# Turning the last results of a row-wise cosine similarity into rows with block transposes, and awaiting the stores at the last barrier

## The chip, the cores and the metric

The kernel runs on one core of a Trainium2 chip. The time is the device time of one execution in microseconds (us), as a median over runs; "span" is the length of a profiled execution from its first to its last instruction, 1.8 to 2.0 us shorter than the time. In this text PE is TensorE, DVE is VectorE, ACT is ScalarE, POOL is GpSimd and SP is the Sync engine; a "q" behind a name (SPq) means an instruction that the engine's sequencer handles by itself. A "mark" of an engine is a value of its semaphore that others wait for.

## The reference

```python
def setup_inputs():
    return {
        "x": np.random.randn(8192, 8192).astype(np.float32),
        "y": np.random.randn(8192, 8192).astype(np.float32),
    }

def reference(x, y):
    x_norm = np.linalg.norm(x, axis=1, keepdims=True)
    y_norm = np.linalg.norm(y, axis=1, keepdims=True)
    return np.sum(x * y, axis=1) / (x_norm.squeeze() * y_norm.squeeze() + 1e-8)
```

Two matrices of 268 MB each are read once; 8192 numbers are written.

## The kernel before

Rows lie on partitions. ScalarE squares and sums (`square`), VectorE multiplies and sums (`dot`). A loop takes the first 7680 rows in 30 groups of 256; then come four blocks of 128 rows (`NB = 4`), the last of them cut into 13 pieces so that little is left to do when its last piece lands. Every row's result is at first one number on its own partition, a column of 128; to be stored in long pieces it must become a row. The parts that matter here:

```python
    def dot(a, b, acc, into, init=0.0):
        return nc.vector.tensor_tensor_reduce(
            out=into, in0=a, in1=b, scale=1.0, scalar=init, op0=ALU.mult, op1=ALU.add,
            accum_out=acc)
# ... for the pieces of a block:
                chained = b == last and n == len(pieces[b]) - 1
                if not chained:
                    acc = parts[:, XX if p.which == "x" else YY, p.i:p.i + 1]
                    xy, init = parts[:, XY, p.i:p.i + 1], 0.0
                else:                      # the very last piece starts from the sum of the others
                    dve.wait(*marks)
                    m_base = dve.done(nc.vector.tensor_reduce(
                        out=base, in_=parts, axis=AX.X, op=ALU.add))
                    acc, xy, init = fin, bsum[:, XY, b:b + 1], base[:, XY:XY + 1]
# ... after the pieces: norms of the last block on ScalarE, then
        pe.wait(identity, m_dot)
        m_xy = pe.done(nc.tensor.transpose(out=psl[0], in_=bsum[:, XY, :], identity=ident))
        act.wait(m_xy)
        m_dots = act.done(nc.scalar.copy(out=dots, in_=psl[0]))
        dve.wait(m_xn, m_yn)
        mk = dve.done(nc.vector.tensor_scalar(            # the denominator
            out=bden[:, last:], in0=bnorm[:, 1, last:], scalar1=bnorm[:, 0, last:],
            scalar2=EPS, op0=ALU.mult, op1=ALU.add))
        dve.wait(mk)
        mk = dve.done(nc.vector.reciprocal(out=bden[:, last:], in_=bden[:, last:]))
        pe.wait(m_den, mk)
        mk = pe.done(nc.tensor.transpose(out=psl[1], in_=bden, identity=ident))
        dve.wait(mk, m_dots)
        mk = dve.done(nc.vector.tensor_mul(out=orl, in0=psl[1], in1=dots))
        sp.wait(mk)
        stored_last = (sem("stored_last"), 16)
        nc.sync.dma_start(
            out=out.rearrange("(t p) -> t p", p=P)[nt - NB:, :], in_=orl).then_inc(
                stored_last[0], 16)
        sp.wait(stored, stored_last)
```

A function that runs over the finished program moves that last wait to the head of the closing block, in which the engines meet at two barriers and GpSimd clears the semaphores between them.

## Time and profile before

| before | |
|---|---|
| time, median of 3 runs | 1249.45 us (1249.18 to 1249.65) |
| span of the profiled run | 1247.6 us |
| read from HBM | 536.87 MB, 430 GB/s over the span |
| VectorE, ScalarE busy | 56%, 73% |
| last load landed | 1243.07 us |
| from there to the end, "the tail" | 4.51 us |

How to read it: the DMA row of the page stands at 9 (90% or more) in every slice but the last, and no engine is near 100%. The loads set the time up to the landing of the last piece. Only the tail is left for a change of this kind, so I measure everything from the last landing; the landing itself moves between 1242.8 and 1243.6 us from profile to profile, and hides changes of a few tenths in the total time.

Two lines will matter later. The first is the last store's issue, from the view of the output tensor (duration in ns: least, median, most); it was known when predicting. The second, from the view of the line that ends the body, is Sync's drain behind it, whose length the prediction does not use. The line above it is a NOP, Sync's last record in the body; its last start, 1246.2, serves as a cut through the tail later.

```profile
L384 SPq DMA_DIRECT2D out_dram<-orl x1: 348/348/348, 1245.4 to 1245.4; - x1
```

```profile
L168 SPq NOP  x2: 13/16/18, 0.8 to 1246.2; - x2
L168 SPq DRAIN  x1: 90/90/90, 1245.9 to 1245.9; - x1
```

The issue takes 0.35 us, and Sync passes its drain 0.09 us after reaching it.

### The profile page before, as it was taken

How to read it: one execution, taken by the hardware profiler on the slowest of the kernel's cores; microseconds unless marked ns; L12 is line 12 of the kernel's file. 1: busy time of each engine (PE TensorE's matmuls, PEld its weight loads, DVE VectorE, ACT ScalarE, POOL GpSimd, SP SyncE). 2: the span in 40 equal slices, each digit the busy share in tenths (PEclk: the TensorE clock that was granted, in tenths of full speed). 3: DMA queues.
4: the chain of work that ended last, by engine and by line, in shares of the span. 5: the costliest groups of instructions: out<-in, count | busy, mean ns of one | idle time of the engine just before them, and what ended most of it. 6: DMA issues, size and time to landing. Idle time of an engine off the chain costs nothing. (4 is left out here: it accounts for less than half of the span.)

```text
span 1247.6 us, 1785 instructions
## 1 busy us (share of the span) xinstructions
PE 1.3 (0%) x4; PEld 0.3 (0%) x4; DVE 698.2 (56%) x252; ACT 916.9 (73%) x285; POOL 0.8 (0%) x8
## 2 busy tenths in 40 slices
PE   0000000000000000000000000000000000000000
PEld 0000000000000000000000000000000000000000
DVE  1654576545765447654467544675446755457566
ACT  3686776867768668677686776867868668677888
POOL 0000000000000000000000000000000000000000
DMA  9999999999999999999999999999999999999998
GB/s 435 431 414 435 437 437 437 437 435 435 433 412 437 437 437 437 437 437 435 435 424 420 437 437 437 437 437 437 433 433 412 437 437 437 437 437 437 418 425 335
DMA packets 11575, 536.93 MB, mean 430 GB/s; under 512 B 1299, under 2 KB 1845, under 8 KB 2613
## 3 DMA queue, kind: packets, MB, share of 16 engines
q1 hardware_dynamic: 11528, 536.88, 99.6%
q10 hardware_dynamic: 45, 0.03, 0.0%
q14 instruction: 2, 0.02, 0.0%
HBM read 536.87 MB, written 0.03 MB: 430 GB/s over the span
## 5 line engine op out<-in xcount | busy, mean ns | idle before, releaser
L142 ACT ACTIVATE junk<-slot 128x8192 uint8<-128x8192 f32 (+4 forms) x138 | 900.8, 6528 | 326.2 <-ACTq L139 320.5
L145 DVE CUSTOM_DVE_ANT_0 slot<-slot,slot 128x4096 f32<-128x4096 f32 (+1 forms) x60 | 391.1, 6556 | 452.4 <-DVEq L139 452.4
L212 DVE COPY side<-slot 128x4096 f32<-128x4096 f32 x30 | 132.8, 4428 | 71.7 <-DVEq L139 71.7
L145 DVE CUSTOM_DVE_ANT_0 side<-side,slot,part 128x4096 f32<-128x4096 f32 x30 | 134.6, 4488 | 0.0
L145 DVE CUSTOM_DVE_ANT_0 slot<-slot 128x8192 f32<-128x8192 f32 (+3 forms) x5 | 29.6, 5944 | 20.4 <-ACT junk L142 12.7
L142 ACT ACTIVATION_READ_ACCUMULATOR junk<-slot (+1 forms) x138 | 25.7, 186 | 0.0
L145 DVE CUSTOM_DVE_ANT_0 vjunk<-slot 128x384 uint8<-128x384 f32 (+4 forms) x8 | 6.8, 886 | 1.0 <-DMA slot<-in_y_dram 1.0
L145 DVE DVE_READ_ACCUMULATOR2_ANT gsum<- x60 | 6.7, 112 | 0.0
L145 DVE DVE_READ_ACCUMULATOR2_ANT part<- 128x1 f32 x30 | 2.5, 83 | 0.0
L192 ACT ACT_TABLE_LOAD x1 | 1.3, 1283 | 1.0 <-SPq L168 1.0
L350 PE MATMUL side<-ident,gden 128*30 128x128 f32 x2 | 0.6, 395 | 1196.9 <-DVE gden L344 1196.9
L194 ACT ACT_TABLE_LOAD x1 | 1.3, 1283 | 0.1
L145 DVE DVE_READ_ACCUMULATOR2_ANT parts<- 128x1 f32 x11 | 0.9, 82 | 0.0
L353 DVE COPY orow<-side 30x128 f32<-30x128 f32 x2 | 0.5, 279 | 0.6 <-PE side L350 0.6
L371 ACT COPY dots<-side 4x128 f32<-4x128 f32 x1 | 0.3, 254 | 0.7 <-PE side L369 0.7
L145 DVE CUSTOM_DVE_ANT_0 vjunk<-slot,base 128x384 uint8<-128x384 f32 x1 | 0.6, 619 | 0.1
L381 DVE TENSOR_TENSOR orl<-side,dots 4x128 f32<-4x128 f32 x1 | 0.3, 279 | 0.5 <-PE side L379 0.5
L270 DVE RECIPROCAL gden<-gden 128x60 f32<-128x60 f32 x1 | 0.5, 529 | 0.0
L350 PEld LDWEIGHTS side<-ident,gden 128*30 128x30 f32 x2 | 0.1, 107 | 1196.8 <-issue 1196.8
L369 PE MATMUL side<-ident,bsum 128*4 128x128 f32 x1 | 0.4, 373 | 46.9 <-DVE bsum L145 46.9
L379 PE MATMUL side<-ident,bden 128*4 128x128 f32 x1 | 0.4, 374 | 0.0
L340 ACT ACTIVATE gnorm<-gsum 128x120 f32<-128x120 f32 x1 | 0.3, 302 | 0.0
(25 smaller groups left out, 4.4 us busy)
## 6 DMA issues: line engine op xcount, KB each, us to landing
slot<-in_x_dram SPq DMA_DIRECT2D x3, 4096.0 KB, 29.9
slot<-in_y_dram SPq DMA_DIRECT2D x2, 4096.0 KB, 32.2
slot<-in_y_dram SPq DMA_DIRECT2D x1, 2368.0 KB, 35.8
slot<-in_x_dram SPq DMA_DIRECT2D x1, 1984.0 KB, 32.3
slot<-in_y_dram SPq DMA_DIRECT2D x1, 1728.0 KB, 39.4
slot<-in_y_dram SPq DMA_DIRECT2D x1, 1600.0 KB, 35.7
slot<-in_x_dram SPq DMA_DIRECT2D x1, 1088.0 KB, 37.9
slot<-in_y_dram SPq DMA_DIRECT2D x1, 640.0 KB, 40.2
```

The costliest lines, as they stand in the source:

```text
L142: return nc.scalar.activation(out=into, in_=src, func=ACTF.Square, accum_out=acc)
L145: return nc.vector.tensor_tensor_reduce(out=into, in0=a, in1=b, scale=1.0, scalar=init, op0=ALU.mult, op1=ALU.add, accum_out=acc)
L192: nc.scalar.memzero(dummy).then_inc(squared, 1)
L194: nc.scalar.sqrt(out=dummy, in_=dummy).then_inc(squared, 1)
L212: nc.vector.tensor_copy(out=side, in_=xt[:, CUT:])
L270: return dve.done(nc.vector.reciprocal(out=den, in_=den))
L340: m_norm = act.done(nc.scalar.activation(out=gnorm, in_=flat(gsum)[:, 0:2], func=ACTF.Sqrt))
L350: mk = pe.done(nc.tensor.transpose(out=t, in_=gden[:, j:2 * G:2], identity=ident))
L353: rows.append(dve.done(nc.vector.tensor_copy(out=orow[:, :, j], in_=t)))
L369: m_xy = pe.done(nc.tensor.transpose(out=psl[0], in_=bsum[:, XY, :], identity=ident))
L371: m_dots = act.done(nc.scalar.copy(out=dots, in_=psl[0]))
L379: mk = pe.done(nc.tensor.transpose(out=psl[1], in_=bden, identity=ident))
```

## The change

Its intent is to shorten the tail: no trip through TensorE and PSUM for the last results, the three earlier blocks out of the way before the tail, no reduction in front of the last dot, and the store's landing awaited beside the closing barriers and not ahead of them. The core of the diff (cut where marked):

```diff
-    closing = blocks[-1]
+    waits = []
     for b in blocks:
# ... collects the waits for "stored" from all blocks
+    closing = list(blocks[-1].instructions)
+    at = max(n for n, i in enumerate(closing)
+             if i.opcode == "Drain" and i.engine == waits[0].engine)
+    blocks[-1].instructions = closing[:at] + waits + closing[at:]
# ...
+    bcol = sb.tile([P, NB, TB], FP32, name="bcol")          # TB = 32
+    brow = sb.tile([P, NB, TB], FP32, name="brow")
+    stored = nc.alloc_semaphore("stored")                   # one for all three stores
# ...
+        def store_blocks(a, b):
+            dve.wait(m_bcol)
+            m = dve.done(nc.vector.tensor_mul(
+                out=bcol[:, a:b, 0], in0=bsum[:, XY, a:b], in1=bden[:, a:b]))
+            dve.wait(m)
+            m = dve.done(nc.vector.transpose(
+                out=brow[:, a:b].rearrange("p b i -> p (b i)"),
+                in_=bcol[:, a:b].rearrange("p b i -> p (b i)")))
+            sp.wait(m)
+            nc.sync.dma_start(
+                out=out.rearrange("(t q i) -> q t i", i=TB, q=P // TB)[
+                    :, nt - NB + a:nt - NB + b],
+                in_=brow[0:P:TB, a:b]).then_inc(stored, 16)
# ... the chained last dot goes; all pieces are summed by one reduction
-                    m_den = reciprocal(bnorm[:, :, 0:last], bden[:, 0:last], m_norm, m_sum)
-            if b in manys and b != last:
+                    reciprocal(bden[:, 0:last], bnorm[:, :, 0:last], m_norm)
+                    store_blocks(0, last)
+            if b in manys:
# ... at the end: both transposes on TensorE, the copy and the multiply by rows go
+        dve.wait(dve.done(nc.vector.reciprocal(out=bden[:, last:], in_=bden[:, last:])))
+        store_blocks(last, NB)
+        take(nc.sync, stored, 48)
```

A block transpose of a column puts 32 of its values in a row on partitions 0, 32, 64 and 96: the store reads `brow[0:P:TB]`.

More of the change, by code (lines that the diff above doesn't have):

```diff
@@ L28, in first_load_and_last_wait @@
     opening.instructions = head[:at] + [load] + head[at:]
-    closing = blocks[-1]
+    waits = []
     for b in blocks:
-        waits = [i for i in b.instructions
-                 if i.sync_info and any(
-                     "stored" in (w.ant_name or "") for w in i.sync_info.on_wait)]
-        if waits:
-            b.instructions = [i for i in b.instructions if i.name not in {w.name for w in waits}]
-            closing.instructions = waits + list(closing.instructions)
+        own = [i for i in b.instructions
+               if i.sync_info and any(
+                   "stored" in (w.ant_name or "") for w in i.sync_info.on_wait)]
+        if own:
+            waits += own
+            b.instructions = [i for i in b.instructions if i.name not in {w.name for w in own}]
+    assert waits
+    closing = list(blocks[-1].instructions)
+    at = max(n for n, i in enumerate(closing)
+             if i.opcode == "Drain" and i.engine == waits[0].engine)
+    blocks[-1].instructions = closing[:at] + waits + closing[at:]
 class Queue:
@@ L87 @@
     CUT = 2 * K - SIDE
+    TB = 32
     xg = x[0:G * 2 * P, :].rearrange("(r a p j) k -> r a p (j k)", a=SLOTS, p=P, j=2)
@@ L117 @@
     bden = sb.tile([P, NB], FP32, name="bden")
-    base = sb.tile([P, 3], FP32, name="base")
-    fin = sb.tile([P, 1], FP32, name="fin")
+    bcol = sb.tile([P, NB, TB], FP32, name="bcol")
+    brow = sb.tile([P, NB, TB], FP32, name="brow")
     ident = sb.tile([P, P], FP32, name="ident")
@@ L122 @@
     orow = sb.tile([G, P, 2], FP32, name="orow")
-    dots = sb.tile([NB, P], FP32, name="dots")
-    orl = sb.tile([NB, P], FP32, name="orl")
     def sem(name):
         return tc.alloc_semaphore(name)
+    stored = nc.alloc_semaphore("stored")
     landed = [sem(f"landed{s}") for s in range(SLOTS)]
@@ L256, with reciprocal @@
             if ny > 1:
-                m = max(len(pieces[b]) - ny, ny - 1 if b == NB - 1 else ny)
+                m = max(len(pieces[b]) - ny, ny)
                 parts = sb.tile([P, 3, m], FP32, name=f"parts{b}")
                 manys[b] = parts, pool.done(nc.gpsimd.memset(parts, 0.0))
+        m_bcol = pool.done(nc.gpsimd.memset(bcol, 0.0))
         ring = {"A": Ring(junk, act), "V": Ring(vjunk, dve)}
-        def reciprocal(norm, den, squared, dotted):
-            dve.wait(squared, dotted)
+        def reciprocal(den, norm, *marks):
+            dve.wait(*marks)
             m = dve.done(nc.vector.tensor_mul(out=den, in0=norm[:, 0], in1=norm[:, 1]))
@@ L269, in reciprocal @@
             dve.wait(m)
-            return dve.done(nc.vector.reciprocal(out=den, in_=den))
+            dve.wait(dve.done(nc.vector.reciprocal(out=den, in_=den)))
+        def store_blocks(a, b):
[11 more added lines that the diff above has]
+                in_=brow[0:P:TB, a:b]).then_inc(stored, 16)
         def flat(t):
@@ L293 @@
             for n, p in enumerate(pieces[b]):
-                chained = b == last and n == len(pieces[b]) - 1
-                if not chained:
-                    acc = parts[:, XX if p.which == "x" else YY, p.i:p.i + 1]
-                    xy, init = parts[:, XY, p.i:p.i + 1], 0.0
-                else:
-                    dve.wait(*marks)
-                    m_base = dve.done(nc.vector.tensor_reduce(
-                        out=base, in_=parts, axis=AX.X, op=ALU.add))
-                    acc, xy, init = fin, bsum[:, XY, b:b + 1], base[:, XY:XY + 1]
+                acc = parts[:, XX if p.which == "x" else YY, p.i:p.i + 1]
+                xy = parts[:, XY, p.i:p.i + 1]
                 zero = [m_zero] if m_zero else []
@@ L315 @@
                     dve.wait(p.mark, *zero, *[q[0] for q in xmarks],
-                             *([q[1] for q in xmarks] if over else []),
-                             *([m_base] if chained else []))
+                             *([q[1] for q in xmarks] if over else []))
                     if over:
-                        mk_dot = dve.done(dot(p.x, p.src, xy, p.x, init))
+                        mk_dot = dve.done(dot(p.x, p.src, xy, p.x))
                     else:
-                        mk_dot = ring["V"].done(
-                            dot(p.x, p.src, xy, ring["V"].room(p.w), init))
+                        mk_dot = ring["V"].done(dot(p.x, p.src, xy, ring["V"].room(p.w)))
                     marks.append(mk_dot)
-                if chained:
-                    m_fin, m_dot = mk, marks[-1]
                 if b == last and n == 4:
@@ L341 @@
                     out=gnorm, in_=flat(gsum)[:, 0:2], func=ACTF.Sqrt))
-                m_g = reciprocal(gnorm, gden, m_norm, marks[-1])
-                dve.wait(m_g)
+                reciprocal(gden, gnorm, m_norm)
                 m_g = dve.done(nc.vector.tensor_mul(
@@ L353 @@
                     rows.append(dve.done(nc.vector.tensor_copy(out=orow[:, :, j], in_=t)))
-                stored = (sem("stored_groups"), 16)
             if b == 2:
@@ L358 @@
                     out=out[0:G * 2 * P].rearrange("(g q) -> g q", q=2 * P),
-                    in_=orow.rearrange("g p j -> g (p j)")).then_inc(stored[0], 16)
-        psl = [side[0:NB, j * BANK:j * BANK + P] for j in range(2, 4)]
-        act.wait(m_base)
-        m_xn = act.done(nc.scalar.activation(
-            out=bnorm[:, 0, last:], in_=base[:, XX:XX + 1], func=ACTF.Sqrt))
-        act.wait(m_fin)
-        m_yn = act.done(nc.scalar.activation(
-            out=bnorm[:, 1, last:], in_=fin, func=ACTF.Sqrt, bias=base[:, YY:YY + 1]))
-        pe.wait(identity, m_dot)
-        m_xy = pe.done(nc.tensor.transpose(out=psl[0], in_=bsum[:, XY, :], identity=ident))
-        act.wait(m_xy)
-        m_dots = act.done(nc.scalar.copy(out=dots, in_=psl[0]))
-        dve.wait(m_xn, m_yn)
-        mk = dve.done(nc.vector.tensor_scalar(
+                    in_=orow.rearrange("g p j -> g (p j)")).then_inc(stored, 16)
+        act.wait(m_sum)
+        m_norm = act.done(nc.scalar.activation(
+            out=bnorm[:, :, last], in_=bsum[:, 0:2, last], func=ACTF.Sqrt))
+        dve.wait(m_norm)
+        m = dve.done(nc.vector.tensor_scalar(
             out=bden[:, last:], in0=bnorm[:, 1, last:], scalar1=bnorm[:, 0, last:],
             scalar2=EPS, op0=ALU.mult, op1=ALU.add))
-        dve.wait(mk)
-        mk = dve.done(nc.vector.reciprocal(out=bden[:, last:], in_=bden[:, last:]))
-        pe.wait(m_den, mk)
-        mk = pe.done(nc.tensor.transpose(out=psl[1], in_=bden, identity=ident))
-        dve.wait(mk, m_dots)
-        mk = dve.done(nc.vector.tensor_mul(out=orl, in0=psl[1], in1=dots))
-        sp.wait(mk)
-        stored_last = (sem("stored_last"), 16)
-        nc.sync.dma_start(
-            out=out.rearrange("(t p) -> t p", p=P)[nt - NB:, :], in_=orl).then_inc(
-                stored_last[0], 16)
-        sp.wait(stored, stored_last)
+        dve.wait(m)
+        dve.wait(dve.done(nc.vector.reciprocal(out=bden[:, last:], in_=bden[:, last:])))
+        store_blocks(last, NB)
+        take(nc.sync, stored, 48)
 _INS = ['x', 'y']
```

## The prediction

> **What bounds the kernel now.** I read the page's engine row and slices first, then the table of stretches, then the timeline of the last microseconds, then the Sync engine's waits, and last the single semaphore records of the final barrier.
>
> ```profile
> DMA  9999999999999999999999999999999999999998
> HBM read 536.87 MB, written 0.03 MB: 430 GB/s over the span
> core 0: us, PE busy (x) PEld busy (x) DVE busy (x) ACT busy (x) POOL busy (x), PEclk, DMA share, GB/s
> 0.00:1200.00 1200.00, 0.58 (x2) 0.14 (x2) 668.48 (x218) 878.21 (x250) 0.80 (x8) 1.00 1.00 433
> 1232.00:1243.00 11.00, 0.00 (x0) 0.00 (x0) 9.97 (x20) 10.74 (x19) 0.00 (x0) 1.00 0.90 348
> 1243.00:1248.00 5.00, 0.70 (x2) 0.16 (x2) 1.59 (x8) 1.29 (x6) 0.00 (x0) 1.00 0.00 0
> ```
>
> Loads fill the transfer engines for 1243 of the 1247.6 us: DMA share 1.00 at 433 GB/s up to 1200, while VectorE is busy 56% and ScalarE 73% of the span. The change touches no load, no slot and none of the loop's instructions. Whatever it is worth must therefore lie after the last load lands, in the 4.5 us with DMA share 0.00. That tail is 0.36% of the time, so a change of 2% (25 us) isn't to be had there in either direction.
>
> The tail is a serial chain. Its VectorE and TensorE part, from the timeline:
>
> ```profile
> 1242.66 0.55 DVE L145 CUSTOM_DVE_ANT_0 vjunk<-slot 128x384 uint8<-128x384 f32 x1
> 1243.14 0.08 DVE L145 DVE_READ_ACCUMULATOR2_ANT parts<- 128x1 f32 x1
> 1243.33 0.17 DVE L300 TENSOR_REDUCE base<-parts 128x3 f32<-128x21 f32 x1
> 1243.64 0.62 DVE L145 CUSTOM_DVE_ANT_0 vjunk<-slot,base 128x384 uint8<-128x384 f32 x1
> 1244.33 0.37 PE L369 MATMUL side<-ident,bsum 128*4 128x128 f32 x1 [46.88 <-DVE bsum L145]
> 1244.74 0.25 ACT L371 COPY dots<-side 4x128 f32<-4x128 f32 x1 [0.70 <-PE side L369]
> 1245.09 0.28 DVE L381 TENSOR_TENSOR orl<-side,dots 4x128 f32<-4x128 f32 x1 [0.50 <-PE side L379]
> 1245.40 0.35 SPq L384 DMA_DIRECT2D out_dram<-orl  x1
> ```
>
> The last piece's semaphore completes at 1243.071 (landing record). VectorE is then at the end of its self-dot of the last x piece, does the reduction, and only then the last dot, which needs the reduction as its starting value. Transposes on TensorE, a copy, a multiply and the store follow. After the store, from the Sync engine's waits and the summary of the barrier's line:
>
> ```profile
> SPq L55 <- DMA out_dram<-orl: 0.4, 1, 0.4
> L414 POOLq EVENT_SEMAPHORE_RANGE_CLEAR  x1: 222/222/222, 1247.1 to 1247.1; - x1
> ```
>
> Sync stands 0.4 us for the store to land, and only then enters the first of two closing barriers. Between the two, GpSimd clears the semaphores.
>
> **What the Trainium skill says.** "VectorE: DVE Perf Modes", section "The three transpose paths": VectorE transposes 32x32 blocks only, and into SBUF, while TensorE's full transpose goes to PSUM. Before has only the TensorE kind: 0.37 us each, plus 0.25 us for the copy out of PSUM. The same page, "The TRN2 errata", gives (N+151)/0.96 ns for an fp32 two-input operation: 160 ns for 3 elements, 220 for 60. The trace has 159 ns for the multiply of 3 and 0.22 us for that of 60, so it agrees. "Perfetto Trace Analysis", "DMA Instruction — HWDGE", says that the data movement lies outside the issue's recorded window and that confirmation from HBM can take surprisingly long. Here the issue takes 0.348 us and the landing comes 1.203 us after its start (1245.401 to 1246.604). "DMA: Bandwidth & Descriptors", "Specifications", says that pieces under 512 B are read, modified and written. The store before is 4 rows of 512 B; the new last store is 4 rows of 128 B, which no run has shown yet.
>
> **The change part by part.**
>
> 1. *One sum over all pieces.* The last dot no longer waits for the reduction. It needs its data (1243.071) and VectorE, free for the next dot at 1243.14 (the dots before it start 0.48 us apart, as each hands over to its accumulator read). It starts at 1243.14 and not 1243.64: 0.50 earlier. Its sum is out 0.57 later (1242.660 to 1243.234 for its neighbour), at 1243.71; ScalarE's last square is out at 1243.718. The reduction now stands behind both. In the trace it starts 0.09 after the mark that it waits for and signals 0.19 later, so 1243.81 to 1244.00. Then comes one Sqrt of 2 elements for two of 1: 0.02 to start, 0.19 to signal, 1244.21. Before, the second Sqrt had signalled at 1244.044, and VectorE could begin the denominator when the dot was done, at 1244.189. Now it begins at about 1244.24: this part alone gives 0.05 us back.
>
> 2. *Block transposes.* Before, from the denominator's start to the store's issue: 1245.401 - 1244.189 = 1.21 us (scalar operation, reciprocal, TensorE transpose, VectorE multiply). The ScalarE copy of the other transpose ran beside it and ended last (signal 1245.001). Now: scalar operation 0.22 to its signal, reciprocal 0.02 + 0.18, multiply of one column 0.02 + 0.17 (the multiply of 3 takes 159 ns), transpose of 32 elements, start of the issue 0.02. The formula above gives 183/0.96 = 191 ns for 32 elements; I allow 0.22 for filling the block, plus 0.03 to start. Sum 0.22 + 0.20 + 0.19 + 0.25 + 0.02 = 0.88. Issue at 1244.24 + 0.88 = 1245.12, against 1245.40: **0.28 us saved by parts 1 and 2.**
>
> 3. *Three blocks stored on their own.* This adds on VectorE, near 1238.3, a multiply (0.16 + 0.02) and a transpose of 96 elements (247/0.96 = 257 ns, with fill and start 0.31): about 0.5 us in front of the dot of 1280 that began at 1238.15. VectorE sat idle 0.53 us before 1240.15 and 0.43 before 1241.67, both for y pieces, so the delay is absorbed before the tail. The store's 12 rows go behind the loads already issued on the same queue and land near 1243, more than 2 us before the last store is issued.
>
> 4. *Where the stores are awaited.* By the order of the instructions, the wait moves from ahead of both closing barriers to just before Sync's arrival at the second. Sync's last action before it is recorded at 1246.182; the store wait runs at 1246.620, and Sync's next record follows at 1246.688. The other engines need 0.08 to 0.11 us from their corresponding record to their first one in the closing block. So Sync without the wait gets there at about 1246.28, 0.41 earlier. What follows no longer depends on the landing, provided the landing comes before GpSimd is ready at the second barrier. That is 0.54 us after its first release (1246.859 to 1247.401). Counted from the store's issue: first release at +1.05 (1.458 before, less 0.41), GpSimd ready at +1.59; landing at +1.20 and 0.1 us for Sync to react, +1.30. Slack 0.29 us. **0.41 us saved.**
>
> Sum: 0.28 + 0.41 = 0.69 us; 1249.45 - 0.69 = 1248.76, say **1248.8 us**.
>
> **The rivals.**
>
> - *The small rows land late.* If writing 128 B costs more than 0.29 us over 512 B, the second barrier waits for the landing and part of the 0.41 goes: with 0.7 us more, all of it. For it: the page's remark on 512 B. Against: the store's packets took 0.025 us each, and most of the 1.20 us is issue (0.35), start (0.43) and confirmation. Time then 1249.0 to 1249.2.
> - *The chain grows rather than shrinks.* The reduction, Sqrt and two extra VectorE steps are now in series behind the last dot. If the transpose took 0.5 us and each hand-over 0.05 more, parts 1 and 2 would be a loss of about 0.2: 1249.2. Against it: the durations of these sizes are all in the trace, but for the transpose.
> - *VectorE falls behind before the tail.* The added 0.5 us would need a VectorE without gaps from 1238 on; it has 0.96 us of them, so I give this little. It would cost up to 0.3.
> - *Nothing is seen.* The transfers set 1243 us of the time, and the three runs of before spread over 0.47 us (1249.18 to 1249.65). A gain of 0.69 is not far above that, so the difference of medians could come out anywhere from 0.3 to 1.1 faster.
>
> **Range and chances.** The working's own error is about 0.25 us (the transpose's duration, Sync's jump to its closing block, the landing), and the runs add about 0.2 of spread. Leaning towards the rivals, which nearly all cost time, I take 1248.3 to 1249.3. Within 2% is all but certain, as the whole tail is 4.5 us: 0.99.
>
> **What would show it right or wrong.** In the changed profile the last dot should start 0.0 to 0.1 us after the accumulator read of the x self-dot; the 32-element transpose should take 0.19 to 0.25 us; the last store should be issued about 2.05 us after the last landing (before 2.33), and the span should end about 1.77 us after that issue (before 2.18). A Sync wait on the store's landing that ends after GpSimd is ready for the second barrier would show the first rival. An idle time of zero on VectorE before its last four dots would show the third. A load stretch that changes by more than 0.5 us would make the prediction wrong in a way that I didn't work out.

## The result, and the profile after

The changed kernel takes 1249.32 us (median of 6 runs, 1249.14 to 1249.42), the kernel before 1249.43 us (6 runs, 1249.18 to 1249.65). The ratio is 0.9999 with a 95% interval of 0.9986 to 1.0012: the same. The prediction had 1248.8 and a range of 1248.3 to 1249.3; the measured time lies just outside. As the landing of the last piece alone moves by several tenths, the distance to the edge of the range says little; the tail says more.

The stretches show that the loads are untouched and that the tail is still idle of transfers (columns as in the prediction's first fence):

```profile
0.00:1200.00 1200.00, 0.58 (x2) 0.14 (x2) 668.41 (x218) 878.48 (x250) 0.94 (x9) 1.00 1.00 433
1232.00:1243.00 11.00, 0.00 (x0) 0.00 (x0) 10.44 (x22) 10.73 (x19) 0.00 (x0) 1.00 0.88 341
1243.00:1248.00 5.00, 0.00 (x0) 0.00 (x0) 1.67 (x9) 0.96 (x5) 0.00 (x0) 1.00 0.00 0
```

The 0.47 us more of VectorE between 1232 and 1243 are the early multiply and transpose. They are absorbed as foreseen, as the timeline shows: the dot of 1280 begins at 1238.76 (before 1238.15), and the next one at 1240.22 (before 1240.15, after a wait for its data).

```profile
1238.36 0.17 DVE L283 TENSOR_TENSOR bcol<-bsum,bden 128x3 f32<-128x3 f32 x1
1238.56 0.28 DVE L286 STREAM_TRANSPOSE brow<-bcol 128x96 f32<-128x96 f32 x1
1238.76 1.45 DVE L150 CUSTOM_DVE_ANT_0 vjunk<-slot 128x1280 uint8<-128x1280 f32 x1
...
1240.22 1.09 DVE L150 CUSTOM_DVE_ANT_0 vjunk<-slot 128x896 uint8<-128x896 f32 x1
```

The timeline of the tail, from the last dot on (the last piece landed at 1243.118):

```profile
1243.18 0.55 DVE L150 CUSTOM_DVE_ANT_0 vjunk<-slot 128x384 uint8<-128x384 f32 x1
...
1243.85 0.18 DVE L347 TENSOR_REDUCE bsum<-parts 128x3 f32<-128x24 f32 x1
1244.06 0.21 ACT L373 ACTIVATE bnorm<-bsum 128x2 f32<-128x2 f32 x1 [0.30 <-DVE bsum L347]
1244.30 0.21 DVE L376 TENSOR_SCALAR bden<-bnorm 128x1 f32<-128x1 f32 x1 [0.27 <-ACT bnorm L373]
1244.55 0.16 DVE L380 RECIPROCAL bden<-bden 128x1 f32<-128x1 f32 x1
1244.75 0.16 DVE L283 TENSOR_TENSOR bcol<-bsum,bden 128x1 f32<-128x1 f32 x1
1244.94 0.21 DVE L286 STREAM_TRANSPOSE brow<-bcol 128x32 f32<-128x32 f32 x1
1245.18 0.55 SPq L290 DMA_DIRECT2D out_dram<-brow  x1
```

The chain of compute is as predicted: the store is issued 2.06 us after the last landing (predicted 2.05, before 2.33). But its own line has grown from 0.35 to 0.55 us, and Sync's drain behind it, in the view of the line that ends the body, from 90 to 397 ns:

```profile
L173 SPq NOP  x2: 13/16/18, 0.8 to 1246.5; - x2
L173 SPq DRAIN  x1: 397/397/397, 1245.9 to 1245.9; - x1
```

Sync's waits no longer hold a wait of 0.4 us for the last store (the row that the prediction shows has no counterpart); the wait is at the second barrier and finds the stores landed.

The tail can be cut at two of Sync's records: the start of the last store's issue, and Sync's last record ahead of the closing block (the last start of the NOP in the lines above, by which Sync has heard from all engines; here with three decimals from the records themselves). The three stretches add up to the tail:

| us | landing to issue | issue to NOP | NOP to end | tail |
|---|---|---|---|---|
| before | 2.330 | 0.781 | 1.403 | 4.514 |
| after | 2.063 | 1.295 | 0.956 | 4.314 |
| difference | -0.267 | **+0.514** | -0.447 | -0.200 |

The first and the third stretch gained what was foreseen, 0.71 us together. The second one, which the prediction carried over unchanged from the kernel before, took back 0.51. One caution on the first stretch: the kernel before stands in it with a single profile, and four runs below whose code is the same up to the issue (e1, e3, e8, e12) show 2.289 to 2.298, so some 0.035 us of the 0.267 may be chance.

### The profile page after: what moved, and what is told of

Same layout as the page of the kernel before. It is cut to its first block, busy times and chain, and to the rows that moved or that the text cites. A ratio compares the mean times of both kernels' runs of the same rounds, so it can differ in the third digit from the quotient of the medians.

```text
span 1247.4 us, 1781 instructions
## 1 busy us (share of the span) xinstructions
PE 0.6 (0%) x2; PEld 0.1 (0%) x2; DVE 698.6 (56%) x255; ACT 916.6 (73%) x283; POOL 0.9 (0%) x9
```

## The experiments

**Theory A.** The last store has become dear to issue, because its rows lie 32 partitions apart. In the program as it is built, a DMA instruction can carry a mark, a field whose name (`ant_dge_precooked`) speaks of a prepared form. (From here on, "mark" is this field, and not a semaphore's value.) All loads and both stores of the kernel before carry it. Of the changed kernel's DMAs, just the two stores of blocks don't. Building the store in other shapes, without running them, showed where the mark is set: on rows on adjoining partitions (4 rows of 512 or of 128 B, 3 rows, 128 rows of 4 B), and not on rows 2, 32 or 64 partitions apart.

**Rivals.** B: pieces of 128 B in place of 512 B are slow to issue or to land. C: the store is the second on its queue and shares its semaphore with others, and waits for them. A further question was whether the moved wait and the single sum are worth what I reckoned.

The table holds every run's three stretches; the text after it takes them up one by one. Times are medians of the runs, for e9 and e10 of a single one. The kernel before had 1249.44 in the rounds of e1 to e4, 1249.61 in those of e5, e6, e8 and the changed kernel's repeat, and 1249.29 in those of e9 to e12; the three groups ran on three chips. By the verdict at 2% every one of these kernels is "same" (e9 and e10 have no verdict); what tells them apart is the tail. Each tail is read from one profile. Where several profiles hold the same code, landing to issue agrees to about 0.04 us and the stretches behind it to less than 0.02.

| us | landing to issue | issue to NOP | NOP to end | tail | time |
|---|---|---|---|---|---|
| after, again | 2.026 | 1.300 | 0.957 | 4.283 | 1249.67 |
| e1 mark off | 2.289 | 1.458 | 1.303 | 5.050 | 1250.06 |
| e2 rows from partitions 0 to 3 | 2.047 | 0.793 | 0.956 | 3.796 | 1248.78 |
| e3 wait only | 2.296 | 0.785 | 0.956 | 4.037 | 1249.05 |
| e12 the same again | 2.298 | 0.780 | 0.956 | 4.034 | 1248.99 |
| e4 column store | 1.824 | 0.752 | 6.451 | 9.027 | 1253.84 |
| e5 chained | 2.152 | 1.300 | 0.957 | 4.409 | 1249.52 |
| e9 chained, wait later | 1.966 | 1.295 | 0.956 | 4.217 | 1249.28 |
| e6 one store | 2.144 | 1.407 | 0.957 | 4.508 | 1249.32 |
| e8 two marks off | 2.294 | 1.441 | 1.303 | 5.038 | 1250.17 |
| e10 early store marked | 2.059 | 1.384 | 0.956 | 4.399 | 1249.45 |
| e11 by quadrants | 2.533 | 0.795 | 0.956 | 4.284 | 1249.55 |

The changed kernel was run once more as the reference of e5, e6 and e8, and gave the same tail to 0.03 us; its time was 0.35 us longer than in its first six runs. In the two profiled runs, 0.43 us apart, the last load landed 0.46 us later (1243.58 us), which covers the difference.

> The changed kernel once more, as the reference of the three runs beside it on this chip. Tail from the last landing to the end 4.31 us as in its first profile, last store's issue 0.55 us, time 1249.3.

### e1: the kernel before, without the mark on its last store

```diff
+    last = [i for b in blocks for i in b.instructions if i.opcode == "DMACopy"][-1]
+    for b in blocks:
+        b.instructions = [copy.replace(i, ant_dge_precooked=False) if i.name == last.name
+                          else i for i in b.instructions]
```

> The kernel before with one bit changed: the last store (4 rows of 512 B from partitions 0 to 3) loses the mark for the prepared form of issue that the build gives it. Theory A (the changed kernel's last store is slow because its rows lie 32 partitions apart and so has no mark): Sync's issue rises from 0.35 to about 0.55 us, Sync's drain behind it from 0.09 to about 0.40, the landing comes about 1.6 us after the start of the issue (before 1.20), the tail grows by 0.4 us, time about 1249.8. Rival B (rows of 128 B are the cause) and rival C (a second store on the same queue and the shared semaphore): nothing changes, 1249.4.

Nothing else differs: same rows of 512 B, same partitions, one store on the queue. The result is correct and took 1250.06 us (4 runs, 1249.92 to 1250.21; before in the same rounds 1249.44, 1249.11 to 1249.94). The view of the output tensor, and that of the line that ends the body:

```profile
L390 SPq DMA_DIRECT2D out_dram<-orl x1: 757/757/757, 1245.3 to 1245.3; - x1
```

```profile
L174 SPq DRAIN  x1: 352/352/352, 1246.2 to 1246.2; - x1
```

The issue takes 0.76 us in place of 0.35 and the drain 0.35 in place of 0.09; issue to NOP 1.46 in place of 0.78, and the landing comes 1.78 us after the start of the issue in place of 1.20. The mark alone makes the difference; rivals B and C expected no change. (The times, 0.6 us apart, are "same", ratio 1.0005, 0.9988 to 1.0021; the reading rests on the profile.) The size is larger than the 0.51 of the changed kernel, which e6, e8 and e10 take up.

### e2: the changed kernel, its last store reading partitions 0 to 3

```diff
-                in_=brow[0:P:TB, a:b]).then_inc(stored, 16)
+                in_=brow[0:P:TB, a:b] if a == 0 else brow[0:P // TB, a:b]).then_inc(stored, 16)
```

The last block's results are wrong (relative error 0.11). The rows keep their 128 B and their place behind the early store; only the partitions adjoin, so the build sets the mark.

> The changed kernel, its last store reading 4 rows of 128 B from partitions 0 to 3 in place of 0, 32, 64, 96 (the last block's results are wrong on purpose). The build gives this store the mark. Theory A: issue 0.35 us in place of 0.55, end of the span 1.74 us after the start of the issue in place of 2.25, time 0.5 below the changed kernel, about 1248.8. Rivals B and C: 0.55 and 2.25 stay, 1249.3.

```profile
L290 SPq DMA_DIRECT2D out_dram<-brow x2: 308/512/717, 1238.8 to 1245.1; - x2
```

```profile
L173 SPq DRAIN  x1: 133/133/133, 1245.5 to 1245.5; - x1
```

In the first line the shortest, 308 ns, is the last store and 717 ns the unmarked early one. Issue to NOP falls from 1.295 to 0.793, and the time to 1248.78 us (4 runs, 1248.68 to 1248.92). This is the predicted time, though with a landing that moves by tenths the agreement to 0.02 us is partly luck; and the tail of 3.80 us is the predicted one (4.51 - 0.69 = 3.82): with the issue as cheap as the prediction took it to be, the rest of its sum holds. The landing is 1.184 us after the start of the issue, against 1.203 for rows of 512 B in the kernel before, which is against rival B; the early store still went ahead on the queue, which is against rival C. The converse, rows 32 partitions apart with the mark set, was not run. In e1 the rows adjoin and the issue is dear all the same, so the distance isn't needed for the cost.

### e3 and e12: the kernel before, with only the wait moved

```diff
+    stored = nc.alloc_semaphore("stored")
# ... both stores count on it, and the wait goes to just before Sync's last drain, as in the change
-        sp.wait(stored, stored_last)
+        take(nc.sync, stored, 32)
```

> The kernel before with only the wait for the stores moved to the last barrier (one shared semaphore, two stores). My reading: the end comes 0.41 to 0.45 us earlier after the issue of the last store (1.74 to 1.77 in place of 2.18), time about 1249.0. Rival: the barrier takes the wait's place and the end stays at 2.18, 1249.4.

Issue to end is 1.741 us (before 2.184), a gain of 0.44, and NOP to end is 0.956 as in the changed kernel. So part 4 of the change is worth what it was reckoned to be, on its own. The time is 1249.05 us (4 runs, 1248.80 to 1249.49; before 1249.44). It was run once more beside e11:

> The kernel before with only the wait moved, once more, beside the run above on the same chip, to tell which of the two is the shorter: tail 4.04 as in its first profile, time 0.4 below the kernel before.

1248.99 us (4 runs, 1248.81 to 1249.59; before 1249.29), tail 4.034. The tail is 0.48 us shorter than before in both profiles and 0.25 to 0.28 shorter than that of the changed kernel, so by the tail this one part of the change beats both kernels. The ratios' intervals (0.9995, 0.9979 to 1.0012; and 0.9998, 0.9982 to 1.0015) don't tell it from before: at 0.03% the total time is too noisy, and the tail has to be read.

### e4: the last block stored as a column

```diff
-        store_blocks(last, NB)
+        m = dve.done(nc.vector.tensor_mul(
+            out=rcol, in0=bsum[:, XY, last:], in1=bden[:, last:]))
+        sp.wait(m)
+        nc.sync.dma_start(
+            out=out[(nt - 1) * P:].rearrange("(p o) -> p o", o=1), in_=rcol).then_inc(stored, 16)
```

> The changed kernel, its last block stored as a column of 128 partitions x 4 B straight from the multiply, without the transpose of 32 elements; the build gives this store the mark. Theory A and pieces of 4 B that land by 1.45 us after the issue: the issue starts 0.24 us earlier after the last landing (1.82 in place of 2.06), the end 1.74 after it, tail 3.56 in place of 4.31, time about 1248.6. Rival (128 small pieces land late): the end is 1.74 plus the excess of the landing over 1.45, so as much as the changed kernel's time if they take 2.2 us.

A miss. The issue came 0.24 us earlier and was cheap, as expected, but the last of its 16 landing records stands 6.89 us after its start, and Sync waits for it at the second barrier. The time is 1253.84 us. Sync's wait for the stores, which cost nothing in the changed kernel, shows in the view of Sync's waits as 6 us more in the row of the waits that count their semaphore down when they pass (55 of them in place of 54 without a visible wait for stores, 1041.0 us in place of 1035.1):

```profile
SPq L145 <- SPq L145: 1041.0, 55, 52.9
```

Four pieces of 128 B cost no more than four of 512 B (e2), but 128 pieces of 4 B do: the direction of rival B is right at this size. The experiment changed the size and the number of the pieces together, so which of the two makes the late landing is not shown.

### e5 and e9: part 1 undone: the last dot chained again

```diff
+                chained = b == last and n == len(pieces[b]) - 1
# ... as in the kernel before, and at the end
+        dve.wait(m_xn, m_yn, m_dot)
```

> The changed kernel with part 1 undone: the last dot again takes the sum of the earlier pieces as its starting value. My reading: part 1 cost a little, so the denominator begins at 1.12 us after the last landing (changed kernel 1.18), the tail is 0.06 us shorter, 4.25, time 1249.25. Rival (part 1 is a gain, as its aim was): the denominator begins later than 1.18 and the tail grows by 0.1 or more.

The denominator began 1.27 us after the last landing: the rival's number, but by a fault of the experiment. I had put VectorE's wait for the last dot (`m_dot`) ahead of the denominator, which doesn't need it; the kernel before has no such wait there. The wait was moved to just ahead of the multiply:

> The changed kernel with part 1 undone as in the chained run before this one, but with VectorE's wait for the last dot moved from ahead of the denominator to ahead of the multiply, as the kernel before has no such wait there. My reading: the denominator begins 1.08 to 1.12 us after the last landing (chained run 1.27, changed kernel 1.15 to 1.18), the last issue 0.06 to 0.1 us earlier than the changed kernel's, at 1.95 to 2.0, tail 4.2. Rival (part 1 is a gain in itself): the denominator again begins later than 1.18.

```profile
1244.18 0.08 DVE L152 DVE_READ_ACCUMULATOR2_ANT bsum<- 128x1 f32 x1
1244.18 0.21 DVE L392 TENSOR_SCALAR bden<-bnorm 128x1 f32<-128x1 f32 x1
```

The denominator begins together with the accumulator read, 1.091 us after the last landing, and the issue at 1.966. Over all profiles, the denominator begins 1.09 us after the last landing in the six with the chained dot (1.077 to 1.118, leaving out the faulty one) and 1.17 in the seven with one sum that were measured (1.148 to 1.188). So the single sum costs 0.08 us on the way to the denominator; it is a small loss, not a gain. The wait that I had misplaced cost 0.18.

### e6: part 3 undone: one store of all four blocks

```diff
-                    store_blocks(0, last)
-        store_blocks(last, NB)
+        store_blocks(0, NB)
```

> The changed kernel with part 3 undone: no early store, the last store takes all four blocks (16 rows of 128 B), the last transpose is 128 elements. Theory A, with a first issue of the unmarked form dearer than a second one: the transpose takes 0.29 us (0.21), the issue about 0.75 (0.55), the tail grows by about 0.3 to 4.6, time 1249.6. Rival C (the changed kernel's last store is slow because another store went ahead of it on the queue): the issue falls to 0.35 and the tail to 3.9, time 1248.9.

```profile
L290 SPq DMA_DIRECT2D out_dram<-brow x1: 707/707/707, 1245.3 to 1245.3; - x1
```

The tail grows by 0.2 us over the changed kernel's, to 4.51: 0.1 for the transpose of 128 elements, which takes 0.31 us in place of 0.21, and 0.1 for the issue. Rival C expected 0.35 us for the issue and falls again: without a store ahead of it the unmarked issue is no cheaper. The time, 1249.32, is 0.35 below that of the changed kernel in the same rounds, against the tail; the last load landed at 1243.16 in this profile and at 1243.58 in the other.

### e8 and e10: why 0.76 us once and 0.55 another time

In e8 the kernel before lost the mark on the last store and on the load of the last x piece, whose issue starts 16.3 us earlier in the trace, and not some 12 as the expectation has it (the list `off` holds both names in the edit of e1). In e10 the changed kernel's early store read partitions 0 to 3 and so got the mark, with three blocks' results wrong:

```diff
-                in_=brow[0:P:TB, a:b]).then_inc(stored, 16)
+                in_=brow[0:P:TB, a:b] if a else brow[0:P // TB, a:b]).then_inc(stored, 16)
```

> The kernel before with the mark taken off the last store, as in the first of these runs, and also off the load of the last x piece, issued some 12 us earlier. If a first issue of the unmarked form is dearer than a second: the last store's issue takes 0.55 to 0.60 us in place of 0.757, the tail is 0.15 to 0.2 us shorter than 5.05, time 1249.9. Rival (the 0.757 belongs to the rows of 512 B or to adjoining partitions): 0.757 and 5.05 stay, 1250.06.

> The changed kernel, its early store of three blocks reading partitions 0 to 3, so that the build marks it and the last store is the only unmarked one on its queue (results of three blocks are wrong on purpose). If a first unmarked store is dearer than a second: the last store's issue takes 0.70 to 0.76 us in place of 0.55, tail 4.5. Rival (the dearer issues belong to rows of 512 B or to 16 rows): 0.55 and 4.3 stay.

```profile
L290 SPq DMA_DIRECT2D out_dram<-brow x2: 338/494/651, 1238.8 to 1245.1; - x2
```

In e8 the last store's issue took 0.737 us: an unmarked load earlier doesn't make it cheaper. (Whether that load was dearer to issue can't be seen: its issue took 2.03 us, and 2.01 in the kernel before.) In e10 the last store, now the only unmarked DMA on its queue, took 0.651 us in place of 0.552, so half of the 0.2 us goes with an unmarked store ahead of it; this rests on one profile. The other half, between 0.651 and 0.757, stays open: rows of 512 B, or adjoining partitions, or something else. The early unmarked issue of the changed kernel thus made its last one cheaper by 0.1, the opposite of rival C. Nor does the mark alone set the length of an issue: the marked store of the groups, which ScalarE issues, took 0.64 to 0.65 us in every profile.

### e11: a version meant to beat both

```diff
-        store_blocks(last, NB)
+        m = [dve.done(nc.vector.tensor_mul(
+            out=qcol[0:TB, q:q + 1], in0=bsum[q * TB:(q + 1) * TB, XY, last:],
+            in1=bden[q * TB:(q + 1) * TB, last:])) for q in range(2)]
+        act.wait(m_rec, m_qcol)
+        m += [act.done(nc.scalar.activation(
+            out=qcol[0:TB, q:q + 1], in_=bsum[q * TB:(q + 1) * TB, XY, last:],
+            func=ACTF.Copy, scale=bden[q * TB:(q + 1) * TB, last:])) for q in range(2, 4)]
+        dve.wait(*m)
+        m = dve.done(nc.vector.transpose(out=qrow, in_=qcol))
# ... the store reads qrow[0:4]
```

> A kernel meant to beat both: the changed kernel, but the last multiply is done per 32 partitions (two on VectorE, two on ScalarE), each into its own column of partitions 0 to 31, so that one block transpose leaves the four rows on partitions 0 to 3 and the store keeps the mark. Multiplies 0.37 us in place of 0.20, issue 0.35 in place of 0.55, end 1.75 us after it in place of 2.25: tail 3.9 to 4.0, time 1249.0. Rival (moving between groups of partitions is dear): the issue comes 0.5 us or more later than 2.05 after the last landing and the gain is gone.

```profile
1245.10 0.33 DVE L385 TENSOR_TENSOR qcol<-bsum,bden 32x1 f32<-32x1 f32 x2
1245.10 0.61 ACT L389 ACTIVATE qcol<-bsum,bden 32x1 f32<-32x1 f32 x2 [0.48 <-DVE bden L383]
1245.81 0.20 DVE L393 STREAM_TRANSPOSE qrow<-qcol 32x32 f32<-32x32 f32 x1 [0.39 <-ACT qcol L389]
```

The rows get to partitions 0 to 3 and the store keeps its mark (issue 0.31 us), but the two multiplies on ScalarE take 0.61 us, where 0.37 had been reckoned for all four side by side, so the issue begins 2.53 us after the last landing. Part of this could have been known: "ScalarE: Activation LUTs", section "What ACT_TABLE_LOAD costs", gives about 280 ns for an operation with one per-partition operand against 186 without, and an overlap of 93 ns back to back. The trace of the kernel before agrees with the first (0.29 us for the Sqrt with a bias per partition, 0.19 without), and from the page one would estimate 0.47 us for the two; here each took 0.29 us, and the second began 0.025 us after the end of the first, so they didn't overlap. The result is correct, its tail of 4.28 no better than the changed kernel's, and its time 1249.55 us. The better version remains e3.

## Why the prediction was wrong, point by point

**The bound and the size of the stake were right.** The loads set the time, the change was worth tenths of a microsecond, and "within 2%" was sure.

**Part 1 (the single sum) was right**, and so was its sign: predicted to give back 0.05 us, measured 0.06 between the two first profiles and 0.08 over all.

**Part 2 (block transposes) was right.** From the denominator's start to the issue I reckoned 0.88 us; it took 2.063 - 1.181 = 0.88. The transpose of 32 elements took 0.211 us, with 0.22 allowed; to take the two-input formula for it was an estimate. One reading of the kernel before was wrong, without harm to the sum: not ScalarE's copy (signal at 1245.001) ended last before the multiply, but TensorE's transpose of the denominators (1245.040), as the line of the multiply says.

**Part 3 was right.** The added work on VectorE was absorbed by its idle time, and the early store landed at 1243.30, 1.88 us before the last store's issue (reckoned: near 1243, more than 2 us).

**Part 4 is where the step failed.** The gain of the moved wait, 0.41, was right (0.447 from NOP to end, 0.44 alone in e3), and so was the landing not being on the path: it came 1.60 us after the issue, and GpSimd was ready at the second barrier at 2.07. What failed is the sentence that counts from the store's issue, "first release at +1.05 (1.458 before, less 0.41)". It carries over from the kernel before the stretch from issue to NOP, for a store of another shape. That term is missing from the sum: 0.781 us before, 1.295 after, +0.514. With it, 0.69 - 0.51 = 0.18 us, and the tail shortened by 0.20. The first release came at +1.54 and not at +1.05, and the span ended 2.25 us after the issue and not 1.77. e1 (the mark alone, same shape) and e2 (adjoining partitions, with 1248.78 us measured against 1248.8 predicted) show that the unmarked form of issue is the cause.

**The first rival named the wrong mechanism.** It expected the small rows to land late because of their size. They did land 0.39 us later after the issue than before, but because they were sent later: the packets of the last store begin 1.19 us after the start of the issue, where they began at 0.78, and take 0.011 us each (before 0.025). "DMA: Bandwidth & Descriptors", section "Why a DMA increments its semaphore by 16 and not by 1", says that a DMA on fewer than 16 engines has the issuing sequencer write the rest of the increment itself. The trace agrees: each store of four rows has five landing records. The first of them, which I take for the sequencer's own, comes at 0.461 us after the start of the issue before and at 0.968 after, and Sync's drain ends 0.10 and 0.11 us behind it. The same holds in all thirteen profiles whose last store has five records (0.10 to 0.11 us). So the drain is most likely the rest of the dear issue, in another line's name.

**The last rival, that nothing is seen, came true as far as the time goes:** a tail shorter by 0.20 us doesn't stand out of runs that spread over half a microsecond.

## What to carry to other kernels

The price of issuing a DMA went here with the form in which it was built, and the build chose the form by the access pattern: before trusting a duration from the kernel before, check that the new transfer is built in the same form, and in a serial tail look at the issue and the drain behind it as closely as at the arithmetic. A layout that saves 0.3 us of compute can lose more than that, as here 0.51 us, if it leaves the result on partitions that don't adjoin. When a change has several parts, run each alone: here one of them, the moved wait, had more of the gain than the whole.

## What the Trainium skill lacked or had wrong

- "DMA: Bandwidth & Descriptors": no section says that on this chip a store whose rows don't lie on adjoining partitions, and so lacks the mark, is dearer to issue. Issue to NOP: 0.78 us with the mark and 1.46 without it for the same store; 0.79 and 1.30 for the changed kernel's.
- The same page, "Specifications", gives 512 B as the least size for full rate but no cost below it; elsewhere the page has an overhead per packet and a floor for tiny transfers, but no landing times by size. Four pieces of 128 B landed 1.18 us after the start of a marked issue, four of 512 B 1.20; 128 pieces of 4 B took 6.89.
- "VectorE: DVE Perf Modes", "The three transpose paths": it has one figure for VectorE, for 16-bit values (311 ns for 128x128). Here fp32 block transposes on 128 partitions took 0.211 us for 32 elements, 0.279 for 96 and 0.311 for 128 (so as long as the 16-bit one), about 0.02 us over that page's formula for two-input operations.
- "ScalarE: Activation LUTs", "What ACT_TABLE_LOAD costs": the overlap of 93 ns between operations back to back is not seen in e11, where two with a per-partition scale took 0.61 us together. The two Sqrts of the kernel before do overlap, by 0.06 us, so the figure does not hold for every pair.
